# The first modulation in two halves of the features, with TensorE summing a part and ScalarE writing h's high half

## The chip, the core and the metric

The kernel runs on one core of a Trainium2 chip. The core has five engines with an instruction queue each: PE (TensorE, matrix products and transposes into PSUM), DVE (VectorE), ACT (ScalarE), POOL (GpSimd) and SP (SyncE, which here only issues DMAs). In the profile PEld is the part of PE that loads weights. The metric is the device time of one execution, in microseconds (us). The profile comes from one such execution; its span runs from the first to the last instruction.

## The reference

One layer of a hybrid decoder trunk on x (2048 tokens, 1024 features), float32:

```
mod = silu(c) @ W_ada + b_ada        -> sh1, sc1, gt1, sh2, sc2, gt2   (1024 each)
h   = rms_norm(x, g_mix) * (1 + sc1) + sh1
p   = h @ W_in                       -> columns for three mixers: attention, mLSTM, gating
x   = x + gt1 * (concat(mixers) @ W_out)
h   = rms_norm(x, g_ffn) * (1 + sc2) + sh2
x   = x + gt2 * ConvFFN(h)
```

What matters here is the beginning: `sh1` and `sc1` (two rows of 1024 out of `mod`), `h`, and the first columns of `h @ W_in`. `h` and the weights are split into a high and a low half (`hh`, `hl`; `whi`, `wlo`, type fp32r), and a product is the sum of three matmuls, high by high, high by low and low by high.

## The kernel before

Tokens run in four blocks of 512 (`tb` 0 to 3), the projections in two halves of two blocks each, features in eight slices `k` of 128. The program is written in one order; the framework fixes the order of the instructions of each engine before the run and may put an instruction ahead of an earlier written one on the same engine. During the run each engine keeps its order and waits for what an instruction needs.

The start, in written order:

1. `c` is loaded and turned into columns; `cs = silu(c)` has one column per slice (L402).
2. Four x tiles (128 tokens by 1024) are loaded. `norm_x` (L493) squares each on ACT, takes the root on POOL and scales on DVE (L503).
3. `first_mod(0)` (L440): the modulation for the first half of the features, slices 0 to 3. Shift and scale each need a 1024 by 512 part of `W_ada`, loaded as eight row pieces `wa` of 128 by 512 in the buffers with the tag `hT` (L414). `mod_sum` (L417) multiplies each piece by its column of `cs` and adds it up on DVE, one instruction per piece. A matmul with a column of ones (L444) sums over the partitions into PSUM. The sums are turned into `sh1` and `a1 = (1 + sc1) * g_mix`, one column per slice, with the bias from `columns` (L446 to L450).
4. `w_block` (L552) loads the first column block of `W_in` (256 columns of the mLSTM keys and 16 gates, width 272) in two parts of four slices; ACT rounds to `whi` (L569), POOL subtracts for `wlo` (L570; the other column blocks use DVE).
5. `first_mod(1)`: slices 4 to 7 in the same way.
6. `make_h(0)` (L537): for each slice PE transposes the four x tiles (L542) into a PSUM bank, ACT applies scale and shift, `h32` (L546), DVE casts `hh` (L547) and subtracts `hl` (L548). In token block 0 the banks come in turn from the tags `trp` (two banks) and `acc` (three, with `acc2`); later from `trp` alone. `hh` and `hl` take `hT` buffers.
7. `head_setup` (L515): small loads, among them `wsn`, which POOL masks (L525), PE transposes (L531) and ACT copies to `wT` (L532). Then `make_h(1)`, whose x tiles share five buffers (`t4k`) with those of block 0.
8. `natural` (L583) goes through the eight token tiles of a half: 24 matmuls each (L54 to L56) into an `acc` bank, then `use_km` copies the result out. Other column blocks follow. At the half's change `make_h(2)` and `make_h(3)` come, about 440 us into the run.

Of the kernel before, what the change touches and what calls it, by code (L numbers as in the profile page):

```python
# [8 lines left out]
F32 = mybir.dt.float32  # L9
F32R = mybir.dt.float32r  # L10
# [23 lines left out]
def trunk(  # L34
# [341 lines left out]
    def tr_ps():  # L376
        return pp.tile([P, 512], F32, name="trp", tag="trp")
# [4 lines left out]
    def mps():  # L382
        return pp.tile([P, 512], F32, name="mps", tag="mps")
# [30 lines left out]
            dma(st, w_ada[k * P : k * P + P, col : col + 512])  # L414
            yield st

    def mod_sum(tiles):  # L417

        acc = pool.tile([P, 512], F32, name="modacc", tag="t2k")
        for k, st in enumerate(tiles):  # L420
            if k == 0:
                V.tensor_scalar(acc, st, cs[:, 0:1], None, op0=ALU.mult)
            else:
                V.scalar_tensor_tensor(acc, st, cs[:, k : k + 1], acc, op0=ALU.mult, op1=ALU.add)
        return acc
# [9 lines left out]
        V.tensor_scalar(gq8, colA[:, 32:33], 0.125, None, op0=ALU.mult)  # L435


    modp = mps()

    def first_mod(hf):  # L440
        for n in (hf, 2 + hf):
            acc = mod_sum(load_ada(n * 512, "hT"))
            for j in range(4):
                T.matmul(modp[:, n * 4 + j : n * 4 + j + 1], acc[:, j * P : (j + 1) * P], ones[:, 0:1], start=True, stop=True)  # L444
        if hf == 0:
            columns(colA[:, 0:24], 24, g_mix, b_ada[:, 0:2048])  # L446
        sl, o = slice(hf * 4, hf * 4 + 4), hf * 4
        V.tensor_tensor(sh1[:, sl], modp[:, o : o + 4], ba[:, o : o + 4], op=ALU.add)
        V.tensor_tensor(a1[:, sl], modp[:, 8 + o : 12 + o], ba[:, 8 + o : 12 + o], op=ALU.add)
        V.scalar_tensor_tensor(a1[:, sl], a1[:, sl], 1.0, gm[:, o : o + 4], op0=ALU.add, op1=ALU.mult)  # L450

    def rest_of_mod(n):

# [49 lines left out]
            V.tensor_scalar(xt, xt, st, None, op0=ALU.mult)  # L503
        return xin

    x0 = norm_x([load_x(i) for i in range(4)])
    first_mod(0)


    wT = pool.tile([P, 4, P], F32, name="wT")  # L510
# [23 lines left out]

    hT = {}

    def make_h(tb, xin=None):  # L537
        xs = xin if tb == 0 else norm_x(xin or [load_x(tb * 4 + i) for i in range(4)])
        for k in range(KT):
            ps = (tr_ps, acc_ps)[k % 2]() if tb == 0 else tr_ps()  # L540
            for i in range(4):
                T.transpose(ps[:, i * P : (i + 1) * P], xs[i][:, k * P : (k + 1) * P], ident)  # L542
# [3 lines left out]
            A.activation(h32, ps, AF.Identity, bias=sh1[:, k : k + 1], scale=a1[:, k : k + 1])  # L546
            V.tensor_copy(hh, h32)  # L547
            V.tensor_tensor(hl, h32, hh.bitcast(F32), op=ALU.subtract)  # L548
            hT[tb, k] = (hh, hl)


    def w_block(parts, eng=V):  # L552

        width = sum(w for _, w in parts)
        tiles = []
        for kp in range(2):
            st = pool.tile([P, 1088], F32, name="wst", tag="wst")
            hi = pool.tile([P, 1088], F32R, name="whi", tag="whi")
            lo = pool.tile([P, 1088], F32R, name="wlo", tag="wlo")
            n = 4 * width  # L560
            v3 = lambda t: t[:, :n].rearrange("p (a b) -> p a b", a=4)
            o = 0
            for col, wd in parts:
                dma(
                    v3(st)[:, :, o : o + wd],
                    w_in[kp * 512 : kp * 512 + 512, col : col + wd].rearrange("(a p) n -> p a n", p=P),
                )
                o += wd
            A.copy(hi[:, :n], st[:, :n])  # L569
            eng.tensor_tensor(lo[:, :n], st[:, :n], hi[:, :n].bitcast(F32), op=ALU.subtract)  # L570
            tiles += [(v3(hi)[:, a, :], v3(lo)[:, a, :]) for a in range(4)]
        return tiles, width

    pending = []
    background = []
# [7 lines left out]
    def natural(half, wb, consume):  # L583
        tiles, width = wb
        for i in range(8):
            tt = half * 8 + i
            tb, o = tt // 4, (tt % 4) * P
            ps = acc_ps()
            for k in range(KT):
                hh, hl = hT[tb, k]  # L590
                mm3(ps[:, :width], hh[:, o : o + P], hl[:, o : o + P], tiles[k][0], tiles[k][1], k == 0, k == KT - 1)
# [356 lines left out]
    nb = len(blocks)  # L948
    steps = [(h, i) for h in range(2) for i in range(nb)]
    rest = [2, 3, 4, 5, 0, 1, 6, 7]  # L950
    wb = w_block(blocks[0][0], G)
    first_mod(1)
    for n, (half, i) in enumerate(steps):
        if i == 0:
            make_h(half * 2, x0)
            if half == 0:
                head_setup()
            make_h(half * 2 + 1)
        elif n == nb - 1:
            x0 = [load_x(8 + t) for t in range(4)]  # L960
# [14 lines left out]
        cur = wb  # L975
        if n + 1 < len(steps):
            wb = w_block(blocks[steps[n + 1][1]][0])
        blocks[i][1](half, cur)
        if i == 1:
            log_gates(half)  # L980
        if i == 3:
# [634 lines left out]
```

## Time and profile before

| | us |
|---|---|
| three timed runs | 2711.45, 2716.72, 2717.74 |
| their median | 2716.72 |
| the profiled execution | 2712.34 |
| span of the profiled execution | 2710.6 |
| mean granted clock of PE | 0.985 of full speed |

How the views are read. The slices cut the span into 40 equal pieces of 68 us; a digit is the busy share in tenths. In a table by stretch there are, for each engine, the busy us and the number of instructions (x), then PE's granted clock, the share of the DMA engines and the rate in GB/s. A timeline row has the start, the busy time, engine, line, operation, the tile written and those read, the shapes, and how many alike are merged (x); in brackets the engine's idle time before it and what ended that. A row of waits names who waited for whom, the sum in us, how often and the longest. SPq is the issue of DMAs on SP's queue, and not their transfer.

### The profile page before, as it was taken

The page shows a single profiled execution, that of the slowest core. Times are in us where ns is not written, and L with a number is a line of the kernel's source. Part 1 is how long each engine was busy: PE and PEld are TensorE (multiplying, and loading weights), DVE is VectorE, ACT ScalarE, POOL GpSimd, SP SyncE. Part 2 cuts the span into 40 slices and gives each one's busy share as a digit, 9 for nine tenths or more (in the row PEclk, how much of TensorE's full clock was granted, in tenths as well). Part 3 has the DMA queues.
Part 4 walks back from the last instruction along what each step waited for, and adds up shares of the span by engine and source line. Part 5 has one row for each costly group of instructions (what it writes and reads, how often), then busy time and mean ns, then how long its engine had stood idle before and what let it go on. Part 6 is the DMA issues. An engine that isn't in the chain of part 4 may idle for free.

```text
span 2710.6 us, 40295 instructions
## 1 busy us (share of the span) xinstructions
PE 2586.7 (95%) x14345; PEld 2218.3 (82%) x14345; DVE 2005.5 (74%) x3499; ACT 1305.0 (48%) x2452; POOL 453.4 (17%) x592
## 2 busy tenths in 40 slices
PE   6989899989899999999998999999999999999999
PEld 5988788989897877777786888888888888888787
DVE  7455466245457888885659988887988887898797
ACT  4243235243237887884436544444444444444443
POOL 2022222032335665651000000000000000000000
PEclk9989999999999999999999999999999999999999
DMA  7534465324356454525752322227222225849533
GB/s 251 170 89 145 120 186 178 108 52 148 92 144 170 110 142 117 166 63 190 263 206 70 103 82 87 78 86 287 94 85 80 86 79 180 293 135 312 172 104 117
DMA packets 313085, 382.09 MB, mean 141 GB/s; under 512 B 31004, under 2 KB 214264, under 8 KB 310836
## 3 DMA queue, kind: packets, MB, share of 16 engines
q1 hardware_dynamic: 312884, 379.52, 44.3%
q8 instruction: 113, 1.85, 0.3%
q14 instruction: 88, 0.72, 0.1%
HBM read 278.67 MB, written 100.77 MB: 140 GB/s over the span
## 4 chain that ended last, share of the span: by engine, by line
PE 57%; DVE 5%; ACT 2%; DMA 2%; issue 2%; POOL 1%; SPq 0%; DVEq 0%; ACTq 0%; POOLq 0%
PE ub L56 10%; PE ub L54 10%; PE ub L55 10%; PE db L55 4%; PE db L56 4%; PE db L54 4%; PE tp L263 3%; PE sp L210 3%; PE op L249 2%; PE wps L56 2%; PE wps L55 2%; PE wps L54 2%; PE op L250 2%; DVE wspl L1360 1%; ACT L L227 1%
## 5 line engine op out<-in xcount | busy, mean ns | idle before, releaser
L54 PE MATMUL acc<-whi,hh 128*128 128x256 f32 (+1 forms) x1408 | 419.6, 299 | 27.8 <-DVE qn L700 16.9
L56 PE MATMUL acc<-whi,hl 128*128 128x256 f32 (+1 forms) x1408 | 408.7, 292 | 0.1
L55 PE MATMUL acc<-wlo,hh 128*128 128x256 f32 (+1 forms) x1408 | 408.4, 291 | 0.0
L54 PEld LDWEIGHTS acc<-whi,hh 128*128 128x128 f32 x1408 | 278.9, 198 | 34.3 <-ACT ev L694 9.2
L54 PE MATMUL ub<-T,wsph 128*128 128x512 f32 x704 | 274.2, 390 | 5.8 <-ACT wsph L1228 5.8
L55 PEld LDWEIGHTS acc<-wlo,hh 128*128 128x128 f32 x1408 | 278.9, 198 | 0.5 <-issue 0.2
L56 PEld LDWEIGHTS acc<-whi,hl 128*128 128x128 f32 x1408 | 277.8, 198 | 1.0 <-DVE hl L548 0.7
L56 PE MATMUL ub<-T,wspl 128*128 128x512 f32 x704 | 273.7, 389 | 0.4 <-DVE wspl L1229 0.4
L55 PE MATMUL ub<-T,wsph 128*128 128x512 f32 x704 | 273.9, 389 | 0.0
L55 PE MATMUL db<-wspl,wsph 128*128 128x512 f32 x616 | 240.3, 390 | 2.7 <-DVE wspl L1360 2.7
L56 PE MATMUL db<-wsph,wspl 128*128 128x512 f32 x616 | 239.6, 389 | 0.0
L54 PE MATMUL db<-wsph 128*128 128x512 f32 x616 | 238.3, 389 | 0.3 <-ACT wsph L1359 0.3
L1228 ACT CAST wsph<-S 128x512 fp32r<-128x512 f32 x176 | 109.6, 623 | 229.4 <-PE ub L55 164.1
L267 DVE TENSOR_TENSOR plo<-tp,phi 128x512 fp32r<-128x512 f32 (+1 forms) x320 | 187.1, 607 | 34.2 <-ACT phi L266 32.0
L54 PE MATMUL ub<-B,wsph 128*128 128x512 f32 x528 | 207.2, 392 | 2.8 <-ACT wsph L1228 2.8
L56 PE MATMUL ub<-B,wspl 128*128 128x512 f32 x528 | 207.0, 392 | 0.7 <-DVE wspl L1229 0.7
L55 PE MATMUL ub<-B,wsph 128*128 128x512 f32 x528 | 207.1, 392 | 0.0
L227 ACT ACTIVATE L<-L,nm 128x1024 f32<-128x1024 f32 (+2 forms) x192 | 172.4, 902 | 33.0 <-DVE nm L216 30.3
L263 PE MATMUL tp<-ident,L 128*128 128x128 f32 x1088 | 179.6, 277 | 3.9 <-POOL L L232 1.2
L266 ACT CAST phi<-tp 128x512 fp32r<-128x512 f32 (+1 forms) x320 | 160.6, 521 | 44.2 <-PE tp L263 42.9
L210 PE MATMUL sp<-kk,q 128*128 128x512 f32 (+3 forms) x640 | 169.1, 375 | 2.6 <-DVE nm L216 1.6
L232 POOL TENSOR_SCALAR L<-L,rs 128x1024 f32<-128x1024 f32 (+2 forms) x192 | 167.3, 881 | 11.2
(334 smaller groups left out, 5897.5 us busy)
## 6 DMA issues: line engine op xcount, KB each, us to landing
w<-in_w_up_dram SPq DMA_DIRECT2D x88, 512.0 KB
wd<-in_w_down_dram SPq DMA_DIRECT2D x176, 256.0 KB
wa<-in_w_ada_dram SPq DMA_DIRECT2D x96, 256.0 KB
wst<-in_w_in_dram SPq DMA_DIRECT2D x48, 512.0 KB
act_d<-yc SPq DMA_DIRECT2D x44, 512.0 KB
act<-act_d SPq DMA_DIRECT2D x44, 512.0 KB
q<-q_d SPq DMA_DIRECT2D x128, 128.0 KB
hc_d<-hl SPq DMA_DIRECT2D x28, 512.0 KB
```

Of the source, the lines that this page charges most:

```text
L54: T.matmul(ps, lh, rh, start=start, stop=False, skip_group_check=resume)
L55: T.matmul(ps, lh, rl, start=False, stop=False, skip_group_check=resume)
L56: T.matmul(ps, ll, rh, start=False, stop=stop, skip_group_check=resume)
L210: T.matmul(sp[:, b : b + bw], q2[n][:, qs], kk[:, s0 + b : s0 + b + bw], start=n == 0, stop=n == 1 and not last)
L227: A.activation(L[c], L[c], AF.Exp, bias=nm[:, n - 1 : n], scale=-1.0, accum_out=rs[:, c : c + 1])
L232: G.tensor_scalar(t, t, rs[:, 0:1], 1.0, op0=ALU.mult, op1=ALU.mult)
L249: T.matmul(op[:, c0:], vv[:, j, :], hi[:, c0:], start=(j == 0), stop=False)
L250: T.matmul(op[:, c0:], vv[:, j, :], lo[:, c0:], start=False, stop=(j == ns - 1))
L263: T.transpose(tp[:, i * P : (i + 1) * P], rows[i][j // 8][:, (j % 8) * P : (j % 8 + 1) * P], ident)
L266: A.copy(hi[:, c0:], tp[:, c0:])
L267: V.tensor_tensor(lo[:, c0:], tp[:, c0:], hi[:, c0:].bitcast(F32), op=ALU.subtract)
L1228: A.copy(hi, src)
```

## The change

- The loads of a half's sixteen `wa` pieces are a step of their own (`first_load`), apart from the sums. Written order of the loads: x tiles, bias columns, first half of `W_ada`, first part of the first `W_in` block, second half of `W_ada`, second part of the block. Before, both parts stood between the halves, and the bias columns behind the first half.
- `first_mod` has PE multiply pieces 0 and 1 with their columns of `cs` (16 matmuls of one column each per half), and DVE sums pieces 2 to 7. Three sums are added at the end.
- `make_h` can make some of the slices. ACT writes `hh` too, by a second pass over the same PSUM bank, instead of a cast on DVE. This holds for all four token blocks. Slices 4 to 7 of block 0 use the tag `trp` alone.
- The first column block's `wlo` is made by DVE (`split`), not by POOL.
- Written order after that: `first_mod(0)`, slices 0 to 3 of `h`, the first three token tiles' matmuls for these slices (`begun`, 36 matmuls, in three `acc` banks), `first_mod(1)`, the second weight part, slices 4 to 7, `head_setup`, block 1; then the three tiles are completed and the other five follow.

```diff
-    def mod_sum(tiles):
+    def mod_sum(tiles, k0=0):
...
+    def first_load(hf):
+        return [list(load_ada(n * 512, "hT")) for n in (hf, 2 + hf)]
+
+    def first_mod(hf, ws):
+        ps, o = mps(), hf * 4
+        sl = slice(o, o + 4)
+        for i in range(2):
+            for k in range(2):
+                for j in range(4):
+                    c = 8 * i + 4 * k + j
+                    T.matmul(ps[:, c : c + 1], ws[i][k][:, j * P : (j + 1) * P], cs[:, k : k + 1], start=True, stop=True)
+        accs = [mod_sum(w[2:], 2) for w in ws]
+        for i, dst in enumerate((sh1, a1)):
+            V.tensor_tensor(dst[:, sl], ps[:, 8 * i : 8 * i + 4], ba[:, 8 * i + o : 8 * i + o + 4], op=ALU.add)
+            V.tensor_tensor(dst[:, sl], dst[:, sl], ps[:, 8 * i + 4 : 8 * i + 8], op=ALU.add)
+        ps = mps()
+        for i, dst in enumerate((sh1, a1)):
             for j in range(4):
+                T.matmul(ps[:, 4 * i + j : 4 * i + j + 1], accs[i][:, j * P : (j + 1) * P], ones[:, 0:1], start=True, stop=True)
+            V.tensor_tensor(dst[:, sl], dst[:, sl], ps[:, 4 * i : 4 * i + 4], op=ALU.add)
+        V.scalar_tensor_tensor(a1[:, sl], a1[:, sl], 1.0, gm[:, sl], op0=ALU.add, op1=ALU.mult)
...
-    def make_h(tb, xin=None):
+    def make_h(tb, xin=None, ks=range(KT)):
...
-        for k in range(KT):
-            ps = (tr_ps, acc_ps)[k % 2]() if tb == 0 else tr_ps()
+        for k in ks:
+            ps = (tr_ps, acc_ps)[k % 2]() if tb == 0 and ks[0] == 0 else tr_ps()
...
             A.activation(h32, ps, AF.Identity, bias=sh1[:, k : k + 1], scale=a1[:, k : k + 1])
-            V.tensor_copy(hh, h32)
+            A.activation(hh, ps, AF.Identity, bias=sh1[:, k : k + 1], scale=a1[:, k : k + 1])
...
-    wb = w_block(blocks[0][0], G)
-    first_mod(1)
+
+    w0 = [w_get(blocks[0][0], 0)]
+    ws.append(first_load(1))
+    w0.append(w_get(blocks[0][0], 1))
+    first_mod(0, ws[0])
+    make_h(0, x0, range(4))
+    wb = w_split(*w0[0]), 272
+    begun = [acc_ps() for _ in range(3)]
+    for tt in range(3):
+        nat_mm(begun[tt], tt, *wb, range(4))
+    first_mod(1, ws[1])
+    wb = wb[0] + w_split(*w0[1]), 272
     for n, (half, i) in enumerate(steps):
         if i == 0:
-            make_h(half * 2, x0)
             if half == 0:
+                make_h(0, x0, range(4, KT))
                 head_setup()
+            else:
+                make_h(half * 2, x0)
             make_h(half * 2 + 1)
```

`w_get` loads a part of a column block and `w_split` makes its halves (ACT for `whi`, DVE for `wlo`); `nat_mm` is the inner loop of `natural` for some of the slices.

More of the change, by code (lines that the diff above doesn't have):

```diff
@@ L415, in load_ada @@
             yield st
-    def mod_sum(tiles):
+    def mod_sum(tiles, k0=0):
         acc = pool.tile([P, 512], F32, name="modacc", tag="t2k")
-        for k, st in enumerate(tiles):
-            if k == 0:
-                V.tensor_scalar(acc, st, cs[:, 0:1], None, op0=ALU.mult)
+        for k, st in enumerate(tiles, k0):
+            if k == k0:
+                V.tensor_scalar(acc, st, cs[:, k : k + 1], None, op0=ALU.mult)
             else:
@@ L435, in rest_of_columns @@
         V.tensor_scalar(gq8, colA[:, 32:33], 0.125, None, op0=ALU.mult)
[L438 to L442, printed above, removed]
-            for j in range(4):
[L444 to L450, printed above, removed]
+    def first_load(hf):
[14 more added lines that the diff above has]
+        for i, dst in enumerate((sh1, a1)):
+            for j in range(4):
+                T.matmul(ps[:, 4 * i + j : 4 * i + j + 1], accs[i][:, j * P : (j + 1) * P], ones[:, 0:1], start=True, stop=True)
+            V.tensor_tensor(dst[:, sl], dst[:, sl], ps[:, 4 * i : 4 * i + 4], op=ALU.add)
+        V.scalar_tensor_tensor(a1[:, sl], a1[:, sl], 1.0, gm[:, sl], op0=ALU.add, op1=ALU.mult)
     def rest_of_mod(n):
@@ L504, in norm_x @@
         return xin
-    x0 = norm_x([load_x(i) for i in range(4)])
-    first_mod(0)
+    x0 = [load_x(i) for i in range(4)]
+    columns(colA[:, 0:24], 24, g_mix, b_ada[:, 0:2048])
+    norm_x(x0)
+    ws = [first_load(0)]
     wT = pool.tile([P, 4, P], F32, name="wT")
@@ L546, in make_h, with w_get, w_split, w_block @@
             A.activation(h32, ps, AF.Identity, bias=sh1[:, k : k + 1], scale=a1[:, k : k + 1])
-            V.tensor_copy(hh, h32)
+            A.activation(hh, ps, AF.Identity, bias=sh1[:, k : k + 1], scale=a1[:, k : k + 1])
             V.tensor_tensor(hl, h32, hh.bitcast(F32), op=ALU.subtract)
             hT[tb, k] = (hh, hl)
-    def w_block(parts, eng=V):
+    def w_get(parts, kp):
         width = sum(w for _, w in parts)
[L555 to L572, printed above, removed]
+        st = pool.tile([P, 1088], F32, name="wst", tag="wst")
+        v = st[:, : 4 * width].rearrange("p (a b) -> p a b", a=4)
+        o = 0
+        for col, wd in parts:
+            dma(v[:, :, o : o + wd], w_in[kp * 512 : kp * 512 + 512, col : col + wd].rearrange("(a p) n -> p a n", p=P))
+            o += wd
+        return st, 4 * width
+    def w_split(st, n):
+        hi = pool.tile([P, 1088], F32R, name="whi", tag="whi")
+        lo = pool.tile([P, 1088], F32R, name="wlo", tag="wlo")
+        split(hi[:, :n], lo[:, :n], st[:, :n])
+        v3 = lambda t: t[:, :n].rearrange("p (a b) -> p a b", a=4)
+        return [(v3(hi)[:, a, :], v3(lo)[:, a, :]) for a in range(4)]
+    def w_block(parts):
+        return w_split(*w_get(parts, 0)) + w_split(*w_get(parts, 1)), sum(w for _, w in parts)
     pending = []
@@ L581, in tick, with nat_mm, natural @@
             background.pop(0)
-    def natural(half, wb, consume):
+    def nat_mm(ps, tt, tiles, width, ks=range(KT)):
+        tb, o = tt // 4, (tt % 4) * P
+        for k in ks:
+            hh, hl = hT[tb, k]
+            mm3(ps[:, :width], hh[:, o : o + P], hl[:, o : o + P], tiles[k][0], tiles[k][1], k == 0, k == KT - 1)
+    def natural(half, wb, consume, begun=()):
         tiles, width = wb
@@ L586, in natural @@
             tt = half * 8 + i
[L587 to L591, printed above, removed]
+            if i < len(begun):
+                ps = begun[i]
+                nat_mm(ps, tt, tiles, width, range(4, KT))
+            else:
+                ps = acc_ps()
+                nat_mm(ps, tt, tiles, width)
             tick()
@@ L977, in trunk @@
             wb = w_block(blocks[steps[n + 1][1]][0])
-        blocks[i][1](half, cur)
+        if n == 0:
+            natural(0, cur, use_km, begun)
+        else:
+            blocks[i][1](half, cur)
         if i == 1:
```

1 line of the change is left out of this document (added).

## The prediction

> **What bounds the kernel now.** I read the page first: busy times, the slices, the chain that ended last.
>
> ```profile
> PE 2586.7 (95%) x14345; PEld 2218.3 (82%) x14345; DVE 2005.5 (74%) x3499; ACT 1305.0 (48%) x2452; POOL 453.4 (17%) x592
> ...
> PE   6989899989899999999998999999999999999999
> ...
> PE 57%; DVE 5%; ACT 2%; DMA 2%; issue 2%; POOL 1%; SPq 0%; DVEq 0%; ACTq 0%; POOLq 0%
> ```
>
> PE (TensorE) is the bound nearly everywhere. The change can save time only where PE is not fed, and the first slice (68 us) is the emptiest. So next the busy times by stretch, and whom PE waits for in the first 110 us.
>
> ```profile
> 21.00:29.20 8.20, 2.10 (x9) 1.96 (x9) 5.80 (x10) 2.20 (x2) 5.36 (x2) 1.00 1.09 354
> 29.20:40.39 11.19, 4.53 (x21) 4.13 (x21) 10.84 (x18) 3.00 (x4) 0.00 (x0) 1.00 0.57 191
> 49.30:59.40 10.10, 9.78 (x75) 9.12 (x74) 5.69 (x19) 7.35 (x21) 2.20 (x4) 1.00 0.22 70
> 59.40:76.70 17.30, 17.26 (x135) 16.77 (x135) 11.69 (x24) 9.01 (x15) 0.00 (x0) 1.00 0.41 127
> ...
> PE mps L444 <- DVE modacc L424: 14.3, 3, 6.6
> PE trp L542 <- DVE xt L503: 9.4, 5, 5.6
> ```
>
> Columns: stretch, length, busy PE, PEld, DVE, ACT, POOL, then granted clock, DMA share, GB/s. PE is starved until 40.39 us, waiting for the modulation sums on DVE (VectorE); from 49.3 us on it is full. What is gained is at most what starts the full stretch earlier.
>
> The start-up in order of time, from the timelines of DVE, ACT, POOL, PE and SP:
>
> ```profile
> 22.16 1.10 ACT L569 CAST whi<-wst 128x1088 fp32r<-128x1088 f32 x1 [10.67 <-DMA wst<-in_w_in_dram]
> 22.70 3.67 DVE L424 SCALAR_TENSOR_TENSOR modacc<-wa,cs,modacc 128x512 f32<-128x512 f32 x2
> 23.34 5.36 POOL L570 TENSOR_TENSOR wlo<-wst,whi 128x1088 fp32r<-128x1088 f32 x2 [8.57 <-ACT whi L569]
> 26.42 1.87 PE L444 MATMUL mps<-ones,modacc 128*128 128x1 f32 x8 [5.65 <-DVE modacc L424]
> 29.03 0.16 DVE L450 SCALAR_TENSOR_TENSOR a<-a,colA 128x4 f32<-128x4 f32 x1
> 29.63 5.47 DVE L424 SCALAR_TENSOR_TENSOR modacc<-wa,cs,modacc 128x512 f32<-128x512 f32 x7
> 37.78 0.42 DVE L547 CAST hh<-h 128x512 fp32r<-128x512 f32 x1
> 40.39 0.59 PE L54 MATMUL acc<-whi,hh 128*128 128x272 f32 x1 [0.70 <-ACT h L546]
> 45.16 0.24 DVE L450 SCALAR_TENSOR_TENSOR a<-a,colA 128x4 f32<-128x4 f32 x1
> 45.52 0.78 ACT L546 ACTIVATE h<-trp,sh,a 128x512 f32<-128x512 f32 x1 [5.19 <-DVE a L450]
> 47.53 0.79 ACT L546 ACTIVATE h<-acc,sh,a 128x512 f32<-128x512 f32 x1
> 50.03 0.69 DVE L548 TENSOR_TENSOR hl<-h,hh 128x512 fp32r<-128x512 f32 x1
> ```
>
> The first half's scale is ready at 29.19 us, but DVE turns to the second half's sums, and the first `hh` is made only at 37.78. The second half's scale is ready at 45.40, the last `hl` of the token block at 50.72. Column block one does begin with k = 0 to 3 already (40.39), before the second half is there: that part of the change's words is half done.
>
> **The change, part by part.**
>
> *Sums.* Each half loses four of sixteen DVE steps: 4 x 0.78 = 3.1 us (5.47/7 in the 29.63 row). POOL's `wlo` goes too: beside its 5.36 us the two sums of the 22.70 row took 3.67 us where 1.56 is usual, so 2.1 us come back; DVE gets two splits of the kind in the 59.34 row below instead, 1.2 us each. In their place PE gets 16 one-column matmuls per half, two instructions each: 32 x 0.23 us (1.87/8) = 7.5 us. In the first half the idle of PE hides them (2.10 busy of 8.20 us); without that cover they would cost up to 7.5. In the second half they meet the 36 early matmuls; see below. Four more small steps of 0.16 us on DVE per half (the 29.03 row) come to 0.6.
>
> *First half.* The sixteen pieces are queued ahead of the `w_in` piece that ACT awaited until 22.16; its 0.56 MB at 354 GB/s are 1.6 us, so the last piece is there at about 20.5. One DVE step, 1.9 us of PE, 0.5 us of small DVE work and a little latency: scale ready at about 23.9, 5.3 us earlier. ACT then writes four pairs h32/hh by 29.3 (0.67 us apart: 45.52 to 47.53 in three steps), and PE runs 36 early matmuls.
>
> *Second half.* SP's order loads only one `w_in` piece between the halves. 4.19 MB after 22.16 at the 354 GB/s above end at 34.0, my estimate; the other `w_in` piece at 35.6. DVE has 1.2 (split) + 2.8 (four `hl`) + 9.4 (twelve sums) in the 10.1 us before, so it may be 3 us late at worst. With the same last steps the scale is ready at about 37.2, 8.2 us earlier. ACT's eight passes take 5.4 us, the last `hl` is there at 43.3: 7.4 us earlier than 50.72.
>
> *What is late next: the second token block.* PE would have finished the first block's matmuls by about 48. The next x tiles follow this chain:
>
> ```profile
> 37.88 3.32 SPq L408 DMA_DIRECT2D xt<-in_x_dram  x4
> 43.92 1.48 POOL L525 TENSOR_SCALAR_AFFINE_SELECT wsn<-wsn 128x128 f32<-128x128 f32 x4 [15.22 <-DMA wsn<-in_w_s_dram]
> 50.59 0.59 ACT L532 COPY wT<-mp 128x512 f32<-128x512 f32 x1 [2.28 <-PE mp L531]
> 51.07 0.64 ACT L498 ACTIVATE jk<-xt 128x512 f32<-128x512 f32 x1
> 58.67 0.75 DVE L503 TENSOR_SCALAR xt<-xt,st 128x1024 f32<-128x1024 f32 x1 [0.65 <-POOL st L132]
> 59.34 1.22 DVE L570 TENSOR_TENSOR wlo<-wst,whi 128x1024 fp32r<-128x1024 f32 x1
> 59.85 1.45 ACT L546 ACTIVATE h<-trp,sh,a 128x512 f32<-128x512 f32 x2 [1.17 <-PE trp L542]
> ```
>
> The SP queue is not shorter: x is issued from 37.88 on behind the small loads, and three of the four x buffers wait for transposes of k = 7, which now wait for ACT's passes of k = 5 (37.2 + 2.7, so about 40). `wsn` still lands at 43.9. POOL is done at 45.4, PE and ACT copy `wT` by 46.9, and if ACT keeps its order the squares start there: 4.2 us earlier than 51.07. If the squares go first, they start with the first x tile, a quarter of 2.1 MB after 41.2, so at about 43: a gain of at most 8. The other end is none, if the transposes of k = 7 hold the x loads back by 4 us. I take 4.2, the order in the rows.
>
> *ACT instead of DVE for `hh`.* ACT's pairs take 1.34 to 1.45 us per k (the 59.85 row), DVE's cast and subtraction 1.07 (rows below). In the 59.40:76.70 stretch PE has 17.3 us of work for 8 k, less a fourth tile that comes behind (24 matmuls, about 2.9): 1.8 per k. So PE hides it there; without this cover it is 8 x 0.3 to 0.4 = 2.2 to 3.0 us per token block. In the third and fourth block the cover is thin:
>
> ```profile
> 440.66 0.69 DVE L548 TENSOR_TENSOR hl<-h,hh 128x512 fp32r<-128x512 f32 x1
> 441.73 0.69 DVE L548 TENSOR_TENSOR hl<-h,hh 128x512 fp32r<-128x512 f32 x1
> 444.19 1.30 SPq L408 DMA_DIRECT2D xt<-in_x_dram  x3
> 455.60 0.29 PE L56 MATMUL acc<-whi,hl 128*128 128x272 f32 x1
> 455.90 0.66 PE L542 MATMUL trp<-ident,xt 128*128 128x128 f32 x4
> ```
>
> The x loads at 444.19 wait for the last transposes, these for a bank that ACT now holds for two passes: by 8 x 0.4 about 3.0 us later. Squares, norms and transposes of block four follow. PE ran out of block three's matmuls at 455.9 exactly as block four came; now I count 2.4 us of new idle, the 3.0 less what PE's own later end covers (bounds 0 and 3.0, or 5.0 with the clock below).
>
> *The clock.* A PE gap costs more than itself:
>
> ```profile
> 160.48 0.54 PE L805 MATMUL mps<-ident,R 100*128 100x100 f32 x4 [2.29 <-DVE R L794]
> 162.75 0.41 PE L55 MATMUL acc<-wlo,hh 128*128 128x256 f32 x1
> 162.96 0.41 PE L56 MATMUL acc<-whi,hl 128*128 128x256 f32 x1
> 168.20 0.28 PE L55 MATMUL acc<-wlo,hh 128*128 128x256 f32 x1
> 168.32 0.28 PE L56 MATMUL acc<-whi,hl 128*128 128x256 f32 x1
> 160.00:164.00 4.00, 3.52 (x21) 3.42 (x22) 2.97 (x9) 1.68 (x2) 0.61 (x1) 0.75 0.19 46
> 180.00:184.00 4.00, 4.00 (x19) 3.78 (x19) 2.42 (x7) 1.71 (x3) 1.33 (x2) 0.50 0.00 1
> ```
>
> Behind a gap of 2.29 us matmuls start 0.21 us apart instead of 0.12, and the granted clock falls to 0.75 of a 4 us stretch, later to 0.50. That is 1 to 2 us lost per gap. The new gap before block two (48 to 55) gets 1.6. The Trainium skill, "TensorE: Matmul & The Clock Gate", Part 1, says that the clock halves after about 3.4 us of idling and recovers after as long busy. This speaks against a change that starts PE early and lets it run dry; the trace is harsher, with a gap of 2.29 us enough; by the page's threshold the 2.4 us gap of block four would add nothing, by the row 1 to 2 us.
>
> **The sum.** Block two earlier 4.2, less 1.6 for the clock, less 0.3 for the first `hh` (0.67 on ACT for 0.42 on DVE): 2.3 gained. Third and fourth block: 2.4 lost. Net nothing; with the bounds of each term, from 8 gained to 9 lost. The profiled execution took 2712.3 us (span 2710.6); the three runs have the median 2716.7, and all four a mean of 2714.6. I forecast 2714 for the runs, which is no change. About 0.3% (8.1 us) is what a measurement of this kernel can tell from none.
>
> **Rivals.**
> 1. *The start-up gain passes through*: squares go first, block two comes 8 us earlier, the clock stays up, and PE has other columns ready in block four. For it: 6.6 of 11.19 us idle before 40.39, and the last `hl` of block one 7.4 us earlier. Against: the `wsn` and x loads. 2714.6 - 8 = about 2707. 20%.
> 2. *ACT becomes the bound, slower*: each PSUM bank is held for two ACT passes, so blocks two, three and four are paced by ACT. It decides where ACT's pair with its other work (casts of 1.1 us as in the 22.16 row) exceeds PE's 1.8 per k. Price 3.0 each, without any start-up gain: +9, or 2724. Against: PE was 17.26 of 17.30 busy in block two. 13%.
> 3. *The change doesn't do what it says*: each engine's order is fixed beforehand, as DVE's 29.63 row shows, so sums may still stand ahead of `hl`, or the PE queue may make the second half's sums wait behind the early matmuls (36 x 0.21 + 7.5 = 15 us of PE between 24 and 37). Then nothing is gained and 2.4 lost: 2717. 15%.
>
> Forecast 52%. Tails of it on either side give: faster by over 0.3% 0.23, within 0.63, slower 0.14. The range, down to rival 1 and up to most of rival 2: 2705 to 2724.
>
> **What would show it.** Right: scales written at about 24 and 37 us, first column matmul near 25, last `hl` of block one near 43, then PE idle of several us before block two, whose ACT passes begin near 55; half-rate matmuls behind that gap; a longer wait of transposes for x near 450. Wrong: block two beginning before 52 (rival 1), PE waiting for `hh` inside blocks (rival 2), first column matmul still after 35 (rival 3). A reshuffled order between 160 and 400 us, where PE gaps like that of 2.29 us hang on DVE, could shift the time either way by several us unforeseen.

## The result, and the profile after

| | before | changed |
|---|---|---|
| median of the runs made side by side, us | 2717.23 (4 runs, 2711.45 to 2719.92) | 2739.26 (4 runs, 2736.1 to 2741.58) |
| profiled execution, us | 2712.34 | 2739.88 |
| its span, us | 2710.6 | 2738.2 |
| mean granted clock | 0.985 | 0.980 |

The changed kernel takes 1.0081 times as long, 95% interval 1.0066 to 1.0097: 22 us slower. The forecast was 2714, the range 2705 to 2724; the time lies outside it. The two profiled executions differ by 27.5 us, because the one of before was 4.9 us under its median.

The page of the changed kernel: the span, busy times, PE's slices, the shares of the chain that ended last.

```profile
span 2738.2 us, 40443 instructions
PE 2601.8 (95%) x14409; PEld 2234.4 (82%) x14409; DVE 1990.6 (73%) x3469; ACT 1323.3 (48%) x2484; POOL 449.0 (16%) x590
...
PE   6988888999898999999998999999999999999999
...
PE 55%; DVE 7%; DMA 3%; ACT 2%; issue 2%; POOL 1%; DVEq 0%; SPq 0%; ACTq 0%; POOLq 0%
```

PE is busy 15.1 us longer, about what its 64 more instructions cost (64 x 0.23 = 14.7). That alone is not the loss: kernel 15 below has the same 64 more, is busy for 2600.4 us and takes 0.12% longer than the kernel before, not 0.81%. What it costs beyond that is waiting, and a lower clock (0.980 for 0.985); DVE's share of the chain rises from 5 to 7%. The first slices are not fuller than before. The same start by stretches, cut at the scales and at the gaps (columns: stretch, length, busy PE, PEld, DVE, ACT, POOL, granted clock, DMA share, GB/s):

```profile
21.00:30.68 9.68, 4.63 (x23) 4.55 (x22) 5.06 (x13) 0.00 (x0) 0.00 (x0) 1.00 1.05 379
30.68:36.98 6.30, 6.30 (x31) 6.30 (x31) 1.29 (x2) 6.20 (x9) 0.00 (x0) 1.00 0.59 184
36.98:45.20 8.22, 7.38 (x46) 6.95 (x47) 7.94 (x17) 1.24 (x2) 1.39 (x1) 1.00 0.53 177
45.20:53.78 8.58, 3.61 (x21) 3.49 (x21) 4.47 (x11) 2.71 (x6) 1.42 (x4) 0.61 0.26 77
53.78:69.47 15.69, 11.01 (x59) 9.79 (x60) 9.27 (x21) 11.20 (x26) 2.19 (x4) 0.72 0.45 148
69.47:88.20 18.73, 18.73 (x145) 18.45 (x145) 7.00 (x13) 13.61 (x23) 0.00 (x0) 0.96 0.28 96
```

In the first two stretches DVE, the engine that the start hangs on, is busy for 5.06 of 9.68 and for 1.29 of 6.30 us: it waits. PE then is empty for 5.0 of 8.58 and 4.7 of 15.69 us, and its clock falls to 0.61 and 0.72. In the kernel before it was full from 49.3 us on. The waits and the order, from the timelines of DVE, PE, SP and ACT of the changed kernel:

```profile
18.10 1.44 PE L457 MATMUL mps<-ones,modacc 128*128 128x1 f32 x6 [2.14 <-DVE modacc L424]
19.40 1.84 PE L449 MATMUL mps<-cs,wa 128*128 128x1 f32 x8
21.53 1.85 PE L449 MATMUL mps<-cs,wa 128*128 128x1 f32 x8
23.41 0.16 DVE L452 TENSOR_TENSOR sh<-mps,colA 128x4 f32<-128x4 f32 x1 [5.37 <-PE mps L449]
24.47 3.90 DVE L424 SCALAR_TENSOR_TENSOR modacc<-wa,cs,modacc 128x512 f32<-128x512 f32 x5
30.15 6.97 PE L449 MATMUL mps<-cs,wa 128*128 128x1 f32 x32
30.52 0.16 DVE L459 SCALAR_TENSOR_TENSOR a<-a,colA 128x4 f32<-128x4 f32 x1
34.58 1.29 DVE L136 TENSOR_TENSOR wlo<-wst,whi 128x1088 fp32r<-128x1088 f32 x1 [3.90 <-ACT whi L135]
36.98 0.57 PE L54 MATMUL acc<-whi,hh 128*128 128x272 f32 x1
38.03 0.50 SPq L408 DMA_DIRECT2D xt<-in_x_dram  x1
38.41 0.49 DVE L422 TENSOR_SCALAR modacc<-wa,cs 128x512 f32<-128x512 f32 x1
52.02 0.16 DVE L459 SCALAR_TENSOR_TENSOR a<-a,colA 128x4 f32<-128x4 f32 x1
53.78 1.12 PE L553 MATMUL trp<-ident,xt 128*128 128x128 f32 x4 [1.99 <-ACT hh L558]
56.72 1.30 SPq L408 DMA_DIRECT2D xt<-in_x_dram  x3
69.47 0.78 ACT L557 ACTIVATE h<-trp,sh,a 128x512 f32<-128x512 f32 x1 [3.52 <-PE trp L553]
```

Three things are to be seen. DVE's order has the small adds of PE's products ahead of the second sum (23.41 ahead of 24.47), so DVE stands for 5.37 us, and the first scale is written at 30.68 us. PE's order made the wait long: half of the products, those of the scale by the written order, stood behind the matmuls of the first sum, which had waited 2.14 us for DVE (18.10), and ran from 19.40 to 23.38 only. The add of the shift waited for them too; both lie in one PSUM tile. The second half's sums begin at 38.41, behind `wlo` and the first `hl`; its scale is written at 52.18 (45.40 before). Only one x tile is issued at 38, the other three at 56.72, and the second token block's first ACT pass is at 69.47 (59.85 before).

Where the 27.5 us of the profiled pair come in, read off the ends of column blocks (the end of ACT's last copy out of PSUM): first block 77.05 to 88.20 (+11.2); end of the first half of the projections +15.4; second half's first block +21.2 (5.8 more there); end of the projections +23.9; end of the execution +27.5.

### The profile page after: what moved, and what is told of

Its sections match the earlier page's. It is cut to its first block, busy times and chain, and to the rows that moved or that the text cites. A ratio compares the mean times of both kernels' runs of the same rounds, so it can differ in the third digit from the quotient of the medians.

```text
span 2738.2 us, 40443 instructions
## 1 busy us (share of the span) xinstructions
PE 2601.8 (95%) x14409; PEld 2234.4 (82%) x14409; DVE 1990.6 (73%) x3469; ACT 1323.3 (48%) x2484; POOL 449.0 (16%) x590
## 4 chain that ended last, share of the span: by engine, by line
PE 55%; DVE 7%; DMA 3%; ACT 2%; issue 2%; POOL 1%; DVEq 0%; SPq 0%; ACTq 0%; POOLq 0%
PE ub L56 10%; PE ub L54 10%; PE ub L55 10%; PE db L55 4%; PE db L56 4%; PE db L54 4%; PE tp L263 3%; PE sp L210 3%; PE op L249 2%; PE op L250 2%; DVE wspl L1393 1%; PE wps L56 1%; PE wps L55 1%; PE wps L54 1%; DMA ld<-y_d 1%
## 5 line engine op out<-in xcount | busy, mean ns | idle before, releaser
L232 POOL TENSOR_SCALAR L<-L,rs 128x1024 f32<-128x1024 f32 (+2 forms) x192 | 167.2, 881 | 11.2
```

The lines of the kernel that those rows point to most:

```text
L232: G.tensor_scalar(t, t, rs[:, 0:1], 1.0, op0=ALU.mult, op1=ALU.mult)
```

## The experiments

In the expectations the theories are: A, ACT's second pass paces the token blocks and holds the banks; B, all of the loss is in the waits of the first modulation; C, DVE's small adds wait for PE's products, and these stand ahead of the first column matmuls; D, PE's share is worth having; E, the x loads wait for the last transposes, which have two banks instead of five. F and G are introduced where they came up. "First block" is the end of the first column block against 77.05, "third" that of the second half's first block against 476.08, both in the profiled executions; ratios are those of the timed runs, each with the kernel before on the same chip.

| kernel | second scale | first block | third | median | ratio, 95% interval |
|---|---|---|---|---|---|
| changed | 52.2 | +11.2 | +21.2 | 2739.3 | 1.0081, 1.0066 to 1.0097 |
| 1 changed, hh on DVE | 56.5 | +11.0 | +17.7 | 2730.8 | 1.0046, 1.0028 to 1.0063 |
| 2 before, hh on ACT | 44.2 | +2.1 | +12.7 | 2726.8 | 1.0036, 1.0023 to 1.0049 |
| 3 changed, all sums on DVE | 52.2 | +8.7 | +12.6 | 2728.5 | 1.0041, 1.0026 to 1.0057 |
| 4 changed, one add | 47.1 | +7.0 | +18.6 | 2734.1 | 1.0055, 1.0036 to 1.0075 |
| 5 changed, five banks | 52.3 | +19.0 | +32.2 | 2748.1 | 1.0103, 1.0087 to 1.0120 |
| 6 sums and hh on DVE | 52.4 | +6.7 | +5.7 | 2724.0 | 1.0015, 1.0005 to 1.0025 |
| 7 as 6, five banks | 53.9 | +9.7 | +10.6 | 2729.9 | 1.0042, 1.0027 to 1.0057 |
| 8 as 7, early split | 52.5 | +7.9 | +10.5 | 2727.7 | 1.0037, 1.0025 to 1.0049 |
| 9 as 6, second sums first | 48.4 | +6.7 | +8.1 | 2726.0 | 1.0027, 1.0015 to 1.0039 |
| 10 as 9, PE's share | 51.5 | +10.0 | +18.3 | 2733.4 | 1.0048, 1.0029 to 1.0067 |
| 11 changed, second sums first | 50.5 | +13.6 | +24.0 | 2740.3 | 1.0082, 1.0062 to 1.0102 |
| 12 before, wlo on DVE | 45.5 | +0.1 | +1.0 | 2718.1 | 1.0001, 0.9991 to 1.0011 |
| 13 as 9, five banks | 47.6 | +6.4 | +9.7 | 2724.4 | 1.0022, 1.0011 to 1.0033 |
| 14 as 13, PE's share | 51.2 | +12.4 | +16.9 | 2735.3 | 1.0058, 1.0040 to 1.0075 |
| 15 as 14, one start, one add | 40.1 | +0.3 | +2.4 | 2722.7 | 1.0012, 1.0002 to 1.0022 |
| 16 before, w_s block late | 47.8 | +1.6 | +3.5 | 2716.4 | 0.9995, 0.9986 to 1.0004 |
| 17 as 15, w_s block late | 39.0 | -3.0 | +1.3 | 2718.2 | 1.0002, 0.9994 to 1.0011 |
| 18 as 13, w_s block late | 47.7 | +4.9 | +6.5 | 2722.9 | 1.0019, 1.0009 to 1.0028 |

The three places in time come from one profiled execution each, and that can lie off the median of its kernel: 7.7 us above it for kernel 1 (2738.5), 6.3 above for kernel 2 (2733.1), 4.5 under for kernel 6 (2719.5). They show where a loss comes in; its price is the ratio. In kernel 12, which is no slower, they differ from the kernel before by up to 1.0 us, and so much means nothing.

### hh by ACT: undone, and alone (kernels 1 and 2)

```diff
-            A.activation(hh, ps, AF.Identity, bias=sh1[:, k : k + 1], scale=a1[:, k : k + 1])
+            V.tensor_copy(hh, h32)
```

Kernel 1 has this edit in the changed kernel, kernel 2 its reverse in the kernel before.

> The changed kernel with the cast of hh back on DVE in all token blocks; the rest of the change stays. Theory A (ACT's second pass paces the blocks and holds the transposes' banks): the 6 us that the second half's first column block loses go away, and 2 to 4 us of the 11 us lost by the end of the first block in the first half; about 2730 us. Theory B (the loss is in the waits of the first modulation alone): 2737 or more, and the second half's first block is still 6 us late.

> The kernel before with one edit: hh by a second ACT pass. Theory A: 6 us lost at the second half's first column block and 1 to 4 us in the first half, so 2724 to 2728 us, with the loads of the second half's x tiles issued 3 to 4 us later against the passes of h. Theory B: 2717 us, as before.

Undone, it gives 0.35% back (1.0081 to 1.0046); alone it costs 0.36%, some 10 us. Most of it comes at the half's change: kernel 2 goes from +4.5 ahead of it to +12.7 behind it, 8.2 us in one block. The timelines of SP and ACT of kernel 2 there:

```profile
452.69 1.30 SPq L408 DMA_DIRECT2D xt<-in_x_dram  x3
464.22 0.78 ACT L546 ACTIVATE h<-trp,sh,a 128x512 f32<-128x512 f32 x1 [3.55 <-PE trp L542]
464.90 0.77 ACT L547 ACTIVATE hh<-trp,sh,a 128x512 fp32r<-128x512 f32 x1
...
474.18 0.87 ACT L547 ACTIVATE hh<-trp,sh,a 128x512 fp32r<-128x512 f32 x1
```

The same stretch of the kernel before, ACT's passes of block four:

```profile
455.06 6.23 ACT L546 ACTIVATE h<-trp,sh,a 128x512 f32<-128x512 f32 x8 [2.79 <-PE trp L542]
```

The x loads were at 444.19 before; less the 4.5 that the neighbours have moved they are 4.0 late. That is block three's eight pairs. Then block four's own passes run from 464.22 to 475.05, 10.8 us, where the kernel before took 6.2 (455.06 to 461.29), and nothing hides these 4.6 us, since PE has run out of block three. 4.0 and 4.6 are the 8.2 within half a microsecond. All the kernels of the table bear this out: in the six with hh on ACT (changed, 2, 3, 4, 5 and 11) this block loses 4.7 to 8.4 us, in all the others between 3.1 lost and 0.1 gained.

In the first block the pass costs some 2 us: +2.1 in kernel 2, and 2.0 between kernels 3 and 6 below, which differ in it alone and have their second scale at the same time. In kernel 2 ACT's sixteen passes stand ahead of three copies out there too, and PE waits for a bank, by the waits of PE from 54 to 92 us:

```profile
PE acc L54 <- DVE gates L606: 1.0, 1, 1.0
```

Kernel 1 ends the block at +11.0, no earlier than the changed kernel, but its second scale is 4.3 us later, because the casts stand ahead of the sums on DVE; so that pair cannot tell. Theory A holds, with its main cost at the half's change. For kernel 1 its 2730 us came true (2730.8) with neither part as expected: 0.1 us came back in the first block instead of 2 to 4, and 2.7 of 6 in the second half's. That is luck.

### PE's share of the sums: undone, and with one add (kernels 3, 4 and 6)

Kernel 3 sums all eight pieces on DVE:

```diff
-        for i in range(2):
-            for k in range(2):
-                for j in range(4):
...
-        accs = [mod_sum(w[2:], 2) for w in ws]
+        accs = [mod_sum(w) for w in ws]
```

Kernel 4 lets the products and the sums of six pieces accumulate in the same PSUM columns, with one add for shift and scale together; in this form each column's group has its own start, and the values come out wrong, so only its time is read. Kernel 6 is kernel 3 with the cast to hh on DVE as in kernel 1.

> The changed kernel with all eight row pieces summed on DVE and no products on PE. Theory C (DVE's small adds stand in front of the second sum and wait 5.4 us for PE's products, and 7 us of products stand in front of the first column matmuls on PE): the first scale is written 2 to 4 us earlier than 30.7 us in spite of four more sums, the first column matmul before 34 us, and the kernel gains 2 to 5 us against the changed one. Rival D (PE's share is worth the four sums that it saves per half): it is slower than the changed kernel by 3 us or more.

> The changed kernel with PE's products and the sums' products added up in PSUM, and one add for shift and scale together, so that no small DVE add stands in front of the second sum. Theory C: no wait of 5.4 us on DVE, first scale at 24 to 25 us instead of 30.7, first column matmul 5 us earlier, and 5 to 7 us gained over the changed kernel if what follows moves along; only 0 to 2 us if the x loads of the second token block hold it (theory E: they wait for the last transposes of the first block, which have two banks instead of five).

> The changed kernel with all eight pieces of each sum on DVE and the cast to hh on DVE as well. If PE's share of the sums (10.7 us by itself) and ACT's pass for hh (8.5 us by itself) are separate costs, they add up: 2739.3 - 10.7 - 8.5 = 2720, so 2717 to 2724. If they are one cost seen twice (the same second half made late), it stays at 2727 to 2730.

Eight pieces on DVE are 0.40% better than six (1.0081 to 1.0041, some 11 us): theory D falls. C is right on the waits, but it foretold 2 to 5 us. The first block gives 2.4 us back and the first scale comes 1.7 us earlier (28.97); another 5.1 us come back between the first block and the half's change, where no run shows the cause. With one add and no wait for a product the first scale comes at 24.7 us, close to the 23.9 of the prediction, so the wait was what failed there; but the x loads went out at 51.7 only, and the gain in time was 0.26% where kernel 3 has 0.40%. Kernel 6, at 2724.0, was at the upper end of its 2717 to 2724: the two costs mostly add up, 0.66% of 0.81% together. What is left, 0.15%, is that of the rest of the change, its order and its loads among it: the second scale is at 52.4 us there still, 7.0 late, and the first block ends 6.7 late.

### Five banks for the last transposes (kernels 5, 7 and 8)

```diff
-            ps = (tr_ps, acc_ps)[k % 2]() if tb == 0 and ks[0] == 0 else tr_ps()
+            ps = (tr_ps, acc_ps)[k % 2]() if tb == 0 else tr_ps()
...
-    begun = [acc_ps() for _ in range(3)]
-    for tt in range(3):
-        nat_mm(begun[tt], tt, *wb, range(4))
+    begun = ()
```

Kernel 5 is the changed kernel with this edit, kernel 7 is kernel 6 with it, kernel 8 is kernel 7 with the first `w_split` written ahead of `first_mod(0)`.

> The changed kernel, but the three column tiles begun early are left to the ordinary loop, so the token block's last four transposes can alternate over five PSUM banks instead of two. Theory E (the second token block's x loads wait for the last transposes, and these for two banks that ACT holds for two passes each): the group of three x loads is issued at 41 to 46 us instead of 56.7, the first ACT pass of the second token block begins 5 to 9 us before 69.5, the first column block ends 4 to 8 us before 88.2 and the time is 2731 to 2736. Rival (the late second half of the scale, 52.2 us, is what sets the second token block): the x loads still come earlier, but the first column block ends within 2 us of 88.2 and the time is 2738 to 2742.

> As the kernel with both on DVE, and without the tiles begun early, with five banks for the last four transposes: what remains of the change is the order of loads, columns() before the normalisation, and wlo of the first column block on DVE in place of POOL. Theory E: x loads at 41 to 46 us, and 4 to 8 us are saved on top of the kernel with both on DVE: 2712 to 2717, no different from before. Rival: the remaining parts cost by themselves (wlo on DVE ahead of the second half's sums), then 2720 or more.

> As the one before, with the split of the first column block's first w_in piece written ahead of the first modulation. If the place of that split in ACT's and DVE's order holds up the second half's sums, the second scale comes 1 to 2 us earlier than in the one before and the time is 2 us less; otherwise the two are within 2 us of each other.

Kernels 5 and 7 missed. The early split of kernel 8 brought the second scale 1.4 us earlier, as expected, and the block 1.8; the 2.2 us in the median are within the intervals. Timelines of SP, ACT and PE of kernel 5:

```profile
38.20 2.59 SPq L408 DMA_DIRECT2D xt<-in_x_dram  x4
65.89 0.78 ACT L557 ACTIVATE h<-trp,sh,a 128x512 f32<-128x512 f32 x1 [1.92 <-PE trp L553]
76.56 0.94 ACT L622 COPY ev<-acc 128x256 f32<-128x256 f32 x3
77.56 0.60 PE L54 MATMUL acc<-whi,hh 128*128 128x272 f32 x1 [2.37 <-DVE gates L624]
```

The mechanism of theory E is right: all four x loads go out at 38.20, 18.5 us earlier than the last three of the changed kernel, and the second token block's first ACT pass comes 3.6 us earlier. But the block ends 7.9 later. ACT's order now has the sixteen passes ahead of three evictions (76.56), so PE has no free bank until 77.56; and the early matmuls, done in idle time until then, are missing. The edit as a whole costs, here and in kernel 7 (3.0 us of the block against kernel 6). What the banks are worth beside the early tiles no run shows, since the early tiles hold the same banks.

### The second half's sums first (kernels 9, 10, 11 and 12)

Theory F: the first block waits for the second half's scale, ahead of which the change put the first half's `hl` and `wlo`.

```diff
     first_mod(0, ws[0])
-    make_h(0, x0, range(4))
     wb = w_split(*w0[0]), 272
+    first_mod(1, ws[1])
+    make_h(0, x0, range(4))
     begun = [acc_ps() for _ in range(3)]
...
-    first_mod(1, ws[1])
```

Kernel 9 has it in kernel 6, kernel 10 in kernel 1, kernel 11 in the changed kernel. Kernel 12 is the kernel before with `wlo` of the first column block on DVE (`G` left out in the call of `w_block`).

> The kernel with all pieces and the cast to hh on DVE, with one more edit: the second half's modulation is written ahead of the first half's h, as in the kernel before, so DVE does the second half's sums before the first half's hl. Theory F (the first column block ends when the second half's scale allows it; the change put 7 us of other DVE work ahead of that scale, 52.4 us for 45.4, and gained nothing with the early column matmuls): second scale at 45 to 47.5 us, the first column block ends within 2 us of before's 77.1 instead of 83.7, and the time is 2715 to 2720, no different from before. Rival (load order, columns() or wlo on DVE cost the 6.7 us): the block still ends after 81 and the time stays at 2722 or more.

> The changed kernel with PE's share of the sums kept, the cast to hh on DVE, and the second half's modulation ahead of the first half's h. Theory F with PE's share as a wait of its own: the first scale at 30.7 us as in the changed kernel, the second at 44 to 47, the first column block ends 0 to 3 us after before's 77.1, 2716 to 2722. If the four steps that PE takes off DVE pay once the order is mended: second scale at 41 to 43, the block 2 to 4 us before 77.1, 2711 to 2715, faster than before.

> The changed kernel with that order alone: PE's share and hh by ACT stay. Theory F plus ACT's pace: the second scale at 43 to 46 us, the first column block ends 2 to 6 us after before's 77.1, the second half's first column block loses 6 to 9 us more as in the kernel before with hh by ACT; 2724 to 2731. If ACT's second pass is what sets the first block, it still ends after 85 us and the time is 2735 or more.

> The kernel before, with wlo of the first column block on DVE instead of POOL, nothing else. The trace of before shows two DVE sum steps at 3.67 us beside POOL's wlo where 1.56 is usual, so 2.1 us come back, and two splits of 1.3 us are added: the second scale within 1 us of 45.4 and the time within 3 us of before. Rival: the two splits wait for ACT's whi and the loads ahead of the second half's sums and cost 3 us or more.

F as it stood falls: the scale came 4 us earlier in kernel 9, and the first block did not move (+6.7 in both). Kernels 10 and 11 are no better than their counterparts 1 and changed. Kernel 12 acquits `wlo` on DVE, in the order of the kernel before: no difference. In kernel 9 all four x loads are issued from 37.6 to 53 us, behind transposes that have moved behind the early column matmuls: what the order gave, the x loads took.

### Both at once, and a third holder (kernels 13, 14 and 15)

Theory G: scale and x loads each hold the block. Kernel 13 has the edits of kernels 7 and 9 on kernel 6; kernel 14 is that with PE's share as in the change; kernel 15 accumulates PE's products in PSUM as kernel 4 does, but with one start for the whole bank, so that the full sum is kept:

```diff
+                    T.matmul(ps[:, 4 * i + j : 4 * i + j + 1], ..., start=i + j + k == 0, stop=False, skip_group_check=True)
+        accs = [mod_sum(w[2:], 2) for w in ws]
...
+                T.matmul(ps[:, 4 * i + j : 4 * i + j + 1], ..., start=False, stop=True, skip_group_check=True)
+        V.tensor_tensor(sa1[:, :, sl], r3(ps[:, 0:8]), r3(ba)[:, :, sl], op=ALU.add)
```

> All eight pieces and the cast to hh on DVE, the second half's modulation ahead of the first half's h, no tiles begun early, and five banks for the last four transposes: both suspects mended at once. Theory G (two things each hold the first column block: the scale of the second half and the second token block's x loads, which wait for the last transposes and so for the banks; either alone keeps it at 83.7 to 83.8 us): x loads issued by 43 us, second scale at 45 to 46.5 us, the first column block ends within 1.5 us of 77.1, and the time is 2714 to 2720, no different from before. Rival (a third thing holds it): the block ends after 80 and the time is 2722 or more.

> The same with PE's share of the sums as the change has it (two of eight pieces on PE, small adds). It prices PE's share alone, with nothing else late. Against the one before: if DVE's waits for PE's products cost what they cost in the changed kernel, the first scale is at 30.6 instead of 29, the second 2 to 4 us later than in the one before, the block 2 to 4 us later and the time 2718 to 2724. If four DVE steps less per half pay: the second scale 2 to 3 us earlier and the time 2711 to 2715.

> The same with PE's products left to accumulate in PSUM under the sums of the six pieces, one start for the whole bank, so DVE has one add for shift and scale and waits for no product. Theory: the first scale at 24.7 us as in the kernel with one add, the second at 39 to 42 us, the first column block ends 1 to 4 us before 77.1 and the time is 2708 to 2716. Rival (DMA or the x loads set the block by then): second scale early all the same, but the block ends within 1 us of 77.1 and the time is that of before.

Kernel 13 missed: x was out by 41 us, and the block still ended 6.4 late. Its timelines of DVE, PE and ACT:

```profile
37.80 0.16 DVE L450 TENSOR_TENSOR sh<-mps,colA 128x4 f32<-128x4 f32 x1 [1.56 <-PE mps L449]
56.12 0.60 PE L534 MATMUL mp<-ident,wsn 128*128 128x128 f32 x4
56.75 0.58 ACT L535 COPY wT<-mp 128x512 f32<-128x512 f32 x1 [6.18 <-PE mp L534]
57.65 0.64 ACT L499 ACTIVATE jk<-xt 128x512 f32<-128x512 f32 x1
```

ACT, whose order is fixed, stood 6.18 us at the copy to `wT` behind transposes that now stand late on PE; the squares of the second token block began at 57.65 instead of 51.07. The scale, at 47.6, is 2.2 us late: the add of the shift stands between the two sums in both halves, and DVE waits 1.56 us for PE each time (before, both adds came behind both sums); with `wlo`'s split of 1.3 us ahead of the second half's sums, less the 2.1 us that came back beside POOL, that is 2.3 by this count.

Kernel 14 came out far above its 2718 to 2724 (2735.3). The same place costs more in it, because the products of PE stand ahead of it:

```profile
41.80 0.16 DVE L452 TENSOR_TENSOR sh<-mps,colA 128x4 f32<-128x4 f32 x1 [5.43 <-PE mps L449]
```

5.43 us in the second half, as 5.37 in the first half of the changed kernel, and in the same way: half of the products run from 37.78 to 41.77, behind matmuls of the first sum. Against kernel 13 it is 0.36% slower. Kernel 15 has the same PE work and no add between the sums. Its timelines of DVE and ACT:

```profile
24.40 0.17 DVE L454 TENSOR_TENSOR sa<-mps,colA 128x8 f32<-128x8 f32 x1 [1.96 <-PE mps L452]
39.97 0.16 DVE L455 SCALAR_TENSOR_TENSOR sa<-sa,colA 128x4 f32<-128x4 f32 x1
48.90 0.59 ACT L539 COPY wT<-mp 128x512 f32<-128x512 f32 x1 [5.76 <-PE mp L538]
```

Its scale is at 40.1, 11.0 us earlier than in kernel 14 and 5.3 earlier than before, and it is 0.46% faster than kernel 14. So PE's share is not the cost; DVE's place in line behind it is. Nor is it shown to be a gain: against kernel 13, which has no share, kernel 15 is 0.10% faster with intervals that overlap, though its first block ends 6.1 us earlier. The time missed 2708 to 2716 (2722.7); a wait of 5.76 us stands in the last row.

### The third holder taken away (kernels 16, 17 and 18)

The transposes and the copy of the small `w_s` block, with its load, are written behind `make_h(1)`, in the kernel before (16), in kernel 15 (17) and in kernel 13 (18):

```diff
+    def wt_setup():
         wsn = pool.tile([P, 4, P], F32, name="wsn", tag="sq")
...
             make_h(half * 2 + 1)
+            if half == 0:
+                wt_setup()
```

> The kernel before, with the load, transposes and copy of the small w_s block written behind the second token block's h instead of ahead of it; nothing else. It tests what the second token block hangs on in the kernel before: there ACT's squares begin at 51.07, right behind its copy to wT, though x was issued at 37.88. If ACT's place in line behind wT is what holds them: squares begin at 46 to 49 us, the first column block ends 1 to 5 us before 77.1 and the time is 2711 to 2716. Rival (PE has enough columns of the first token block either way, since its gaps before 77 us are 0.3 us only): the block ends within 1 us of 77.1 and the time does not change.

> The kernel with one start, and the w_s block behind the second token block's h. There ACT stood from 42.4 to 48.9 us at its copy to wT, which waited for PE transposes placed behind 60 column matmuls, and the first column block ended at 77.4 in spite of a second scale at 40.1. If that copy is the third holder: squares begin at 43.5 to 46 us, the block ends 3 to 6 us before 77.1, and the time is 2710 to 2717. Rival (PE's columns or x set it): the block ends after 76 and the time stays at 2720 to 2725.

> The kernel with both suspects mended (second half's sums first, five banks), and the w_s block behind the second token block's h, which takes away the third holder that its trace showed: ACT stood from 50.6 to 56.8 us at its copy to wT. If that is the whole rest: squares begin at 50 to 51.5 us, the first column block ends at 76 to 79 instead of 83.5, and the time is 2714 to 2720. Rival (the scale at 47.6 and the cold matmuls behind it hold the block as well): it ends after 81.

Kernel 17's squares begin at 44.3 and its first block ends 3.0 us before that of the kernel before, the least that its theory gave: the only kernel here that starts faster. It does not end faster, and there the theory missed: -0.2 at the end of the first half, +1.3 at the third block, ratio 1.0002. Kernel 18 missed: 1.5 us gained in the block, since ACT's order then put evictions between the squares, and these wait for PE. Kernel 16 changed nothing that the timing can tell; its profiled start was 2.4 us late for a reason of its own (last section), so the control is clouded in its profile, though not in its time. No version here beats the kernel before.

What stays open: how kernel 17's 3 us got lost between 77 and 437 us, and why every kernel with PE's share, in either form, loses 2.1 to 5.6 us more in that stretch, while the others come out of it between 2.1 better and 2.4 worse. The order of the instructions behind the start differs from kernel to kernel, and no run held it fixed. So the mechanisms at the start and at the half's change are shown; their shares of the 22 us are those of the edits as wholes.

## Why the prediction was wrong

1. *"Four more small steps of 0.16 us on DVE per half come to 0.6"* is the step that failed first. As busy time it is right. The adds of PE's products have to wait for these, and DVE's order has them ahead of the second sum. The wait was 5.37 us, and the scale came at 30.68 instead of 23.9. The prediction asked what hides PE's 7.5 us and found PE's idle; it didn't ask who stands behind the products, nor what the products themselves stand behind (18.10 to 23.38). With one add the same scale came at 24.7, so the rest of that sum was right.
2. *"Scale ready at about 37.2"* (second half): measured 52.18. It took the sums to start as the pieces land, "3 us late at worst". They started at 38.41, behind `wlo`, which waited 3.90 us for ACT, behind four more adds that waited for the 32 products at 30.15, and shared DVE with `hl`. Kernel 15, with no waits for products and the sums ahead of `hl`, reached 40.1.
3. *"Block two earlier 4.2"*: it came 9.6 us later (69.47 for 59.85). The bound "none, if the transposes of k = 7 hold the x loads back by 4 us" saw the right holder and gave it far too little: the loads came 18.7 us after the first. Freed, they showed the next holders in line, ACT's evictions (kernel 5) and the copy to `wT` (kernel 13), which the prediction did know, as "if ACT keeps its order".
4. *"The clock: 1.6"*: gaps of 2.97 and 1.99 us came ahead of 53.78, and two stretches ran at 0.61 and 0.72. The mechanism was right; its price was not measured by itself.
5. *"Third and fourth block: 2.4 lost"*: the mechanism was right, the size was not. It took block three's lateness (3.0, measured 4.0) and forgot block four's own passes, 10.8 us for 6.2 with PE idle: 5.8 us in the changed kernel, 8.2 alone. In the first block it had "so PE hides it there"; the pass cost some 2 us there (kernel 2, and 3 against 6).
6. *The rivals.* The third, "the change doesn't do what it says", had the cause, an order fixed beforehand, though with `hl` ahead of the sums and not the reverse, and its sign "first column matmul still after 35" was there (36.98). It was priced at "nothing gained and 2.4 lost". That was the error of the range: a start that fails does not fall back to the start of before. Each late thing passed on to PE, which before had no slack from 49.3 us on; +11.2 by the first block. The second rival's mechanism was there too, for the most part in the second half.

The sum by the timed runs: PE's share with its adds undone alone gives 0.40% back, hh by ACT 0.35%, both together 0.66% of the 0.81%; the 0.15% left is that of the rest, the order and the loads among it.

## What to carry to other kernels

Moving work from a full engine to an idle one saves nothing if the full engine must fetch the result in the middle of its own queue: put the join behind the last step that doesn't need it, or let it happen where the result lies (here in PSUM, which was worth 0.46% against separate adds). When a start is rearranged, list every in-order queue on the way to the next block, with what stands ahead in it; removing one holder shows the next. Price the failure of a rearrangement by what is then late, not by the gain that fails to come.

## What the runs showed of the hardware that was not expected

*DVE beside POOL.* POOL's two `wlo` splits took 5.36 us in the kernel before and in kernel 16. The eight DVE sum steps around them took 8.26 us in the one and 10.55 in the other, with the same instructions and shapes up to there, and 6.13 in kernel 12, where POOL has no split. The traces show why the price differs: a DVE step that starts together with a split, or inside it, takes 2.9 to 3.1 us instead of 0.75, and the other steps are not slowed. In the kernel before only the last step did so (23.49); in kernel 16 the last two did, one for each split (23.00). So the price was 2.1 to 2.3 us for each step that met a split, and not a rate for the time of overlap; 0.6 us between the two engines decided whether it was paid once or twice. Timelines of DVE, from the kernel before:

```profile
18.10 8.26 DVE L424 SCALAR_TENSOR_TENSOR modacc<-wa,cs,modacc 128x512 f32<-128x512 f32 x8
23.49 2.88 DVE L424 SCALAR_TENSOR_TENSOR modacc<-wa,cs,modacc 128x512 f32<-128x512 f32 x1
```

from kernel 16:

```profile
18.40 10.55 DVE L424 SCALAR_TENSOR_TENSOR modacc<-wa,cs,modacc 128x512 f32<-128x512 f32 x8
23.00 5.96 DVE L424 SCALAR_TENSOR_TENSOR modacc<-wa,cs,modacc 128x512 f32<-128x512 f32 x2
```

and from kernel 12:

```profile
18.15 6.13 DVE L424 SCALAR_TENSOR_TENSOR modacc<-wa,cs,modacc 128x512 f32<-128x512 f32 x8
```

The second row of a pair is a part of the first, asked for by a narrower window.

*PSUM groups.* With a start on each column's own group and the groups of a bank interleaved (kernel 4), the sums came out wrong; with one start for the whole bank (kernel 15) they came out right. That fits a start that touches more than the column it writes, so that a part of the sum is lost; no run looked at the bank itself.

*The clock.* In the changed kernel the matmuls at 55.37 and 55.60 start 0.23 us apart, where 0.12 is full speed by the prediction's rows; ahead of them lie gaps of 2.97 us (the row below) and 1.99 us (53.78). The Trainium skill, "TensorE: Matmul & The Clock Gate", Part 1, has the clock halve after about 3.4 us of idling. The traces here are harsher, as the prediction's row of 2.29 us already was: a single gap there, with PE full up to 158.2 us. Whether the two gaps of the changed kernel act one by one or together no run tells. The timeline of PE in the changed kernel:

```profile
49.21 1.09 PE L542 MATMUL mp<-ident,wsn 128*128 128x128 f32 x4 [2.97 <-issue]
...
55.37 0.43 PE L54 MATMUL acc<-whi,hh 128*128 128x272 f32 x1
55.60 0.43 PE L55 MATMUL acc<-wlo,hh 128*128 128x272 f32 x1
```
